# A hybrid scan and convolution layer: TensorE pinned to its written order, the latent convolution in pairs of quarters with re-laid buffers

## The chip, the cores and the metric

The kernel runs on one core of one Trainium2 chip. The metric is device time in microseconds (us) of one execution, as the median of several runs. The core has five engines with a queue of instructions each: TensorE (PE, matmul; its weight loads are shown apart as PEld), VectorE (DVE), ScalarE (ACT), GpSimd (POOL) and SyncE (SP), which here issues every DMA.

## The reference

One layer runs over 256 context tokens and 2048 latent tokens. Cut to what matters here:

```python
h = rms_norm(x, g_pre) * (1 + scale) + shift
u = h @ w_in                                        # 1024 -> 5664
z, xbc, dt_raw, ga, gb, gsil = split(u)
y_ssd, h_fin = ssd_branch(z, xbc, dt_raw, ...)      # bidirectional scan in chunks of 128 tokens
h = ga * sigmoid(gb)                                # conformer_branch
h = depthwise_conv(h, conv_w, conv_b)               # 31 taps along the rows of the grid
y_conf = silu(layer_norm(h, ln_g, ln_b)) * silu(gsil)
out = concatenate([y_ssd, y_conf]) @ w_out
return x + gate * rms_norm(out, g_post), h_fin
```

The context is a grid of 256 x 1, the latents one of 32 x 64; the convolution runs down the 32 rows, so along the latents it joins tokens that lie 64 apart. Within a scan chunk, `y_diag` is a masked, decayed product of 128 x 128 per head, `y_off` what the state so far adds, and `states` what the chunk adds to the state.

## The kernel before

The 2304 tokens are 18 tiles of 128, two of context and sixteen latent, worked in two halves (tiles 0 to 9, 10 to 17). Every large product is made of three matmuls on operands split into a high and a low part in the type float32r (`mm_cm`, L365: high x high, low x high, high x low, for eight k), each with a moving width of 512 or 256. Call a group of three a k-step. The tiles of these are `xp`, `gb`, `ga`, `sp` and, in the output product, `op`.

Each half goes through `xbc_phase` (the projection that feeds the scan, with a 5-tap convolution) and then through `post` (L862): eight `gab_unit`s (`gb` and `ga`, the gated input of the Conformer branch) and the `silu_unit`s (`sp`). While `post` runs, side work is interleaved by `interleave` and `merge` (L842, L49): after so many k-steps the generators of the scan and of the convolution are advanced by a step each. The scan, `pass_a(i)` (L640), is started for a new tile every seven steps. For tile i it loads rows of cumulated decay (`lb`, spread over all partitions), masks them on GpSimd (`mask`), takes exponentials on ScalarE (`decay`), adds the two directions and multiplies by C·B (`mix`), and then uses TensorE: transposes (`pb`, `px`), `diag` (tile `py`: eight matmuls per group g whose stationary operand is 64 columns wide, four of them for each half hq), `off` (`po`, 128 wide), and `state` (`pst`, split operands again). `carry` updates the state in `Sf`, `close` adds up and stores.

The Conformer convolution of the context is done on VectorE (`ctx_conv`, L572, tile `cg`). That of the latents is done on TensorE (`lat_conv(j)`, L595, for each of eight blocks of 128 channels). It loads the gated input as `cx` from the DRAM buffer `GL`, expands the taps `kd` into block-diagonal matrices in one of two buffers `kbuf` (four ScalarE copies for each of four quarters u, L614), runs eight matmuls of 64 columns for a quarter (tile `cp`), and evicts them with the bias into `cvv`, which is stored to `CVL`. The output stage (L1094 on) reads `CVL` back as `cn` (L1030), normalizes, transposes (`ct`), and multiplies by `w_out`.

PSUM has three banks under the tag "mm" for the large products and five under "ss" for all else. The order of instructions on each engine isn't that of the source: the program is built with a scheduler (`schedule_with_timeline_sim=True`, L1214) that reorders each engine's queue by its own estimate of when operands are ready. So TensorE's order around the side work is the scheduler's: in `post` it puts a small matmul wherever it takes its inputs to be there.

The lines that the steps of the prediction touch: L532 (store to `GL`), L608 (load of `cx`), L614 (expansion), L626 (`cp`), L631 (eviction), L636 (store to `CVL`), L712 (`py`), L719 (`po`), L725 to L727 (`pst`), L763 to L765 (`pb`), L688 (`px`), L665 (`el`, an exponential of `lb`), L668 (mask), L676 (decay), L680 and L681 (the two steps of `mix`), L531 and L542 (evictions of `ga` and `sp`), L1030 and L1033 (`cn` and its statistics).

## Time and profile before

| | |
|---|---|
| median of 3 runs | 1885.21 us (1884.33 to 1887.44) |
| profiled execution, its time | 1890.22 us |
| profiled execution, its span | 1888.5 us |
| mean granted TensorE clock | 0.989 |
| DVE busy, share of the span | 63% |
| ACT busy, share of the span | 44% |
| POOL busy, share of the span | 14% |
| DMA packets under 512 B | 85206 of 290400 |

The span runs from the first instruction to the last; 1.7 us lie around it in the execution's time. A row of the timeline gives the start, the duration, the engine, the line, the operation, the tile written and those read, the shapes, and how many instructions are merged in it; a bracket at its end is the time that the engine stood idle before it, and what ended that. A matmul's duration reaches into the next one, since matmuls are pipelined: the cost of one is the distance from its start to the next one's start. A matmul on plain 32-bit operands shows as two records, a transpose as one. A window's row gives, for a stretch of the span, its length, the busy time of PE, PEld, DVE, ACT and POOL (with instructions), the granted TensorE clock, the mean busy share of the 16 DMA engines, and GB/s.

### The profile page before, as it was taken

To read this page: it belongs to the slowest core of one execution; us is meant where nothing else is said; L and a number is where in the kernel's file an instruction comes from. 1 tells how busy PE (TensorE), PEld (TensorE's weight loads), DVE (VectorE), ACT (ScalarE), POOL (GpSimd) and SP (SyncE) were. 2 spreads that over 40 slices of the span, in tenths; PEclk is the share of its full clock that TensorE was granted. 3 is DMA by queue.
4 is the path that set the end of the run, shared out by engine and by line. 5 is a ranking of instruction groups with operands and counts; after the bars stand their busy time and mean duration, and the time that the engine had idled before them with its cause. 6 is when DMAs were issued, how large, how long until landed. Compare 5 with 4: busy or idle time off the path is not lost.

```text
span 1888.5 us, 26833 instructions
## 1 busy us (share of the span) xinstructions
PE 1827.4 (97%) x9739; PEld 1500.1 (79%) x9739; DVE 1192.4 (63%) x1699; ACT 839.9 (44%) x1786; POOL 264.6 (14%) x351
## 2 busy tenths in 40 slices
PE   7899999999999999999999998999999999999998
PEld 4788887787787888888877776767787888888886
DVE  2487877776545543586596758655438767776762
ACT  3647424443455441744356666664414323222321
POOL 0002001111111100100001111100003233333220
PEclk9999999999999999999999999999999999999999
DMA  8556665564686754445587888987887565555532
GB/s 299 213 199 214 216 217 187 169 219 154 206 274 222 229 204 162 162 154 198 186 184 220 213 228 226 246 213 201 248 262 237 182 183 168 160 171 168 177 104 75
DMA packets 290400, 375.29 MB, mean 199 GB/s; under 512 B 85206, under 2 KB 187478, under 8 KB 290268
## 3 DMA queue, kind: packets, MB, share of 16 engines
q1 hardware_dynamic: 290268, 373.58, 63.9%
q8 instruction: 77, 1.26, 0.3%
q14 instruction: 55, 0.45, 0.1%
HBM read 243.92 MB, written 129.59 MB: 198 GB/s over the span
## 4 chain that ended last, share of the span: by engine, by line
PE 60%; DMA 6%; issue 4%; ACT 3%; DVE 3%; SPq 1%; POOL 1%; POOLq 0%; DVEq 0%; ACTq 0%
PE op L1069 19%; PE sp L370 6%; PE sp L371 6%; PE sp L372 6%; DMA lb<-lt 4%; PE xp L372 2%; PE xp L371 2%; PE xp L370 2%; PE ga L370 1%; PE qo L976 1%; PE ga L372 1%; PE ga L371 1%; PE py L712 1%; PE gb L370 1%; PE gb L372 1%
## 5 line engine op out<-in xcount | busy, mean ns | idle before, releaser
L676 ACT ACTIVATE lb<-lb,WB 128x128 f32<-128x128 f32 x576 | 184.2, 391 | 150.9 <-POOL lb L668 149.0
L370 PE MATMUL sp<-hh,wh 128*128 128x512 f32 (+1 forms) x640 | 239.3, 374 | 1.9 <-DVE sth L542 1.9
L371 PE MATMUL sp<-hl,wh 128*128 128x512 f32 (+1 forms) x640 | 237.6, 371 | 0.0
L372 PE MATMUL sp<-hh,wl 128*128 128x512 f32 (+1 forms) x640 | 237.0, 370 | 0.0
L668 POOL TENSOR_SCALAR_AFFINE_SELECT lb<-lb 128x512 f32<-128x512 f32 x144 | 108.7, 759 | 751.8 <-ACT el L665 393.8
L370 PE MATMUL xp<-hh,wh 128*128 128x512 f32 (+1 forms) x480 | 178.0, 372 | 5.3 <-ACT wh L345 3.4
L371 PE MATMUL xp<-hl,wh 128*128 128x512 f32 (+1 forms) x480 | 178.2, 372 | 0.2 <-DVE hl L291 0.2
L372 PE MATMUL xp<-hh,wl 128*128 128x512 f32 (+1 forms) x480 | 178.1, 371 | 0.0
L467 DVE SCALAR_TENSOR_TENSOR cva<-raw,cwh,cva 128x1280 f32<-128x1280 f32 (+1 forms) x96 | 142.5, 1493 | 15.3 <-ACT cva L461 13.4
L370 PEld LDWEIGHTS sp<-hh,wh 128*128 128x128 f32 x640 | 121.1, 189 | 23.9 <-DVE sth L542 2.3
L372 PEld LDWEIGHTS sp<-hh,wl 128*128 128x128 f32 x640 | 121.1, 189 | 20.7 <-issue 0.2
L371 PEld LDWEIGHTS sp<-hl,wh 128*128 128x128 f32 x640 | 121.1, 189 | 20.3 <-issue 0.5
L370 PE MATMUL gb<-hh,wh 128*128 128x512 f32 (+1 forms) x320 | 121.5, 380 | 6.1 <-DVE gth L531 6.1
L370 PE MATMUL ga<-hh,wh 128*128 128x512 f32 (+1 forms) x320 | 120.2, 376 | 3.2 <-ACT gth L528 3.2
L371 PE MATMUL gb<-hl,wh 128*128 128x512 f32 (+1 forms) x320 | 119.4, 373 | 0.0
L372 PE MATMUL gb<-hh,wl 128*128 128x512 f32 (+1 forms) x320 | 119.3, 373 | 0.0
L372 PE MATMUL ga<-hh,wl 128*128 128x512 f32 (+1 forms) x320 | 118.3, 370 | 0.0
L371 PE MATMUL ga<-hl,wh 128*128 128x512 f32 (+1 forms) x320 | 118.2, 369 | 0.0
L582 DVE SCALAR_TENSOR_TENSOR cg<-cg,cv 128x256 f32<-128x256 f32 x240 | 112.3, 495 | 2.5
L542 DVE SCALAR_TENSOR_TENSOR sth<-sth,sp 128x512 f32<-128x512 f32 (+1 forms) x80 | 50.4, 630 | 96.0 <-ACT sth L541 96.0
L370 PEld LDWEIGHTS xp<-hh,wh 128*128 128x128 f32 x480 | 91.3, 190 | 22.0 <-ACT wh L345 4.1
L680 DVE TENSOR_TENSOR lb<-lb,lb 128x512 f32<-128x512 f32 x72 | 50.2, 697 | 88.6 <-ACT lb L676 55.8
(219 smaller groups left out, 3862.9 us busy)
## 6 DMA issues: line engine op xcount, KB each, us to landing
lb<-lt SPq DMA_DIRECT2D x144, 256.0 KB, 4.6
wr<-in_w_in SPq DMA_DIRECT2D x88, 256.0 KB, 4.9
whd<-wh SPq DMA_DIRECT2D x44, 512.0 KB, 3.2
wld<-wl SPq DMA_DIRECT2D x44, 512.0 KB, 4.6
wh<-whd SPq DMA_DIRECT2D x44, 512.0 KB, 5.7
wl<-wld SPq DMA_DIRECT2D x44, 512.0 KB, 5.6
xT<-xb SPq DMA_DIRECT2D x18, 512.0 KB, 5.6
yp<-yg SPq DMA_DIRECT2D x36, 256.0 KB, 4.8
```

Source lines behind the costliest of these rows:

```text
L370: T.matmul(ps[:, :BN], wh[:, k, :], hh[:, k, :], start=(k == 0), stop=False)
L371: T.matmul(ps[:, :BN], wh[:, k, :], hl[:, k, :], start=False, stop=False)
L372: T.matmul(ps[:, :BN], wl[:, k, :], hh[:, k, :], start=False, stop=(k == KT - 1))
L467: V.scalar_tensor_tensor(a[:, :n], raw[:, t:t + n], cwh[:, ct * 5 + t:ct * 5 + t + 1], a[:, :n], MUL, ADD)
L542: V.scalar_tensor_tensor(th, th, 1.0, ps[:, :BN], ADD, MUL)
L582: V.scalar_tensor_tensor(acc, g[:, t:t + 256], cv[:, w0 + t:w0 + t + 1], acc, MUL, ADD)
L668: G.affine_select(E[g, hq, d], E[g, hq, d], pattern=[[0, 4], [sg, P]], compare_op=ALU.is_ge, fill=NEG, base=0, channel_multiplier=-sg)
L676: S.activation(lb[:, h, :], lb[:, h, :], AF.Exp, bias=WB[:, i, c + h:c + h + 1])
L680: V.tensor_tensor(a, a, E[g, hq, 1], ADD)
L712: T.matmul(py[g][j * HD:(j + 1) * HD, q * P:(q + 1) * P], xt[g][:, h * HD:(h + 1) * HD], E[g, hq, 0][:, t, :], start=True, stop=True)
L976: T.matmul(po[:, q * P:(q + 1) * P], Sb[g][:, q * P:(q + 1) * P], ct[:, g, :], start=True, stop=True)
L1069: T.matmul(pso[n], lhs[:, k % 8, :], w[:, n * 512:(n + 1) * 512], start=(k == 0 and m == 0), stop=(k == 15 and m == 2))
```

## The change

1. TensorE's instructions go through a wrapper that, while `T.on` is set, ties each one behind the one written before it, so the scheduler can't move them. It is set over the interleaved stretch of both `post` phases. The other engines are still scheduled freely.
2. `pass_a` is cut into other steps. The two halves of a group's `diag` and its `off` now stand together; the two `px` stand with `pb`; masks, decays, sums and products of `mix` have steps of their own, ahead of the matmul that needs them. A step of `lat_conv` is called right behind `off(0)` and behind `state(1, 0)`. The first context tile to carry its state out gets ten steps instead of seven.
3. `lat_conv` is one generator over the eight blocks. It works in pairs of quarters, has four `kbuf` buffers instead of two and two `cx` buffers instead of one, and expands the taps of block j + 1 right after the pair of block j that used the buffers.
4. `GL` is split: the context part `GLC` as it was, the latent part `GLX` in the order in which `cx` lies in SBUF. So each `ga` block of latents is stored by four DMAs in pieces of 256 B, and `cx` is one DMA of whole rows. `CVL` is written as `cvv` lies (one DMA of whole rows instead of two in pieces of 256 B), and `cn` is read from it by two DMAs in pieces of 256 B, instead of one in rows of 4 KB.
5. The load of the initial state is issued earlier for the first use, `ctx_conv` and `gate_rows` get two empty steps ahead of their matmuls, and the step counts of the interleaving follow.

```diff
+class InOrder:
+    def __init__(self, tc, eng):
+        self.tc, self.eng, self.on = tc, eng, False
+
+    def _put(self, ins):
+        return self.tc.keep_in_program_order(ins) if self.on else ins
+
+    def matmul(self, *a, **k):
+        return self._put(self.eng.matmul(*a, **k))
...
-    V, S, G, T, DMA = nc.vector, nc.scalar, nc.gpsimd, nc.tensor, nc.sync
+    V, S, G, T, DMA = nc.vector, nc.scalar, nc.gpsimd, InOrder(tc, nc.tensor), nc.sync
...
-            DMA.dma_start(GL[j][:, o:o + BN], th)
+            if b == 0:
+                DMA.dma_start(GLC[j], th)
+                continue
+            r0 = (o - NCTX * P) // 64
+            for c4 in range(4):
+                DMA.dma_start(GLX[j][c4 * 32 + r0:c4 * 32 + r0 + BN // 64, :].rearrange("r (g w) -> g r w", w=64),
+                              th.rearrange("(g c) (r w) -> c g r w", c=4, w=64)[c4])
...
-        x = lp.tile([P, 32, 64], F32, tag="cx", name=f"cx{j}", bufs=1)
-        src = GL[j][:, 256:].rearrange("(g c) (r w) -> c r g w", c=4, w=64)
-        for c4 in range(4):
-            DMA.dma_start(x[c4 * 32:(c4 + 1) * 32], src[c4])
...
-        expand(0)
-        yield
-        for u in range(4):
-            kt = kbuf[u % 2]
-            ps = bank("ss", f"cp{j}_{u}")
...
-            if u < 3:
-                expand(u + 1)
-            yield
...
+        def load_g(j):
+            x[j] = lp.tile([P, 32, 64], F32, tag="cx", name=f"cx{j}", bufs=2)
+            DMA.dma_start(x[j].rearrange("p g w -> p (g w)"), GLX[j])
...
+        for j in range(8):
+            vt[j] = lp.tile([P, 32, HD], F32, tag="cvv", name=f"cvv{j}", bufs=1)
+            for v in range(2):
+                ps = [part(j, 2 * v + e) for e in range(2)]
+                for e in range(2):
+                    evict(j, 2 * v + e, ps[e])
+                if j < 7:
+                    if v == 0:
+                        load(j + 1)
+                    else:
+                        load_g(j + 1)
+                    for e in range(2):
+                        expand(j + 1, 2 * v + e)
+                else:
+                    pass
+                if v == 1:
+                    DMA.dma_start(CVL[j * P:(j + 1) * P, :], vt[j].rearrange("p r c -> p (r c)"))
+                yield
...
         diag(0, 0)
+        diag(0, 1)
         off(0)
-        state(0, 0)
-        weigh(1, 0)
-        mix(1, 0)
-        decay(1, 1)
-        yield
-        diag(0, 1)
-        state(0, 1)
-        carry(0)
-        weigh(1, 1)
-        mix(1, 1)
+        if cpg is not None:
+            next(cpg, None)
+        weigh(0, 1)
+        both(1)
+        yield
+        close(0)
+        state(0, 0)
+        times(1)
+        yield
+        carry(0)
+        state(0, 1)
+        weigh(1, 0)
...
-    interleave(post(0, 6), merge(scan(range(9)), 68, extra, 9 + 4 * 13), 90 * 8)
+    T.on = True
+    blocks = post(0, 6)
+    run(take(blocks, 40))
+    interleave(blocks, merge(scan(range(9)), 76, extra, 11 + 4 * 15), 90 * 8 - 40)
+    T.on = False
...
-    kbuf = [lp.tile([P, 8, P], F32, name=f"kbuf{u}") for u in range(2)]
+    kbuf = [lp.tile([P, 8, P], F32, name=f"kbuf{u}") for u in range(4)]
...
+    T.on = True
     run(take(blocks, 24))
-    interleave(take(blocks, 24), [sc_] * 4, 24)
-    interleave(take(blocks, 344), merge(sc_, 63, extra, 8 * 6 + 4 * 13), 344)
+    interleave(take(blocks, 16), [sc_] * 3, 16)
+    next(cpg)
+    interleave(take(blocks, 352), merge(sc_, 68, extra, 4 * 15), 352)
...
-        DMA.dma_start(n, CVC[i * P:(i + 1) * P, :] if i < 2 else CVL[(i - 2) * P:(i - 1) * P, :])
+        if i < NCTX:
+            DMA.dma_start(n, CVC[i * P:(i + 1) * P, :])
+        else:
+            for e in range(2):
+                DMA.dma_start(n[e * 64:(e + 1) * 64, :].rearrange("w (j c) -> w j c", c=64),
+                              CVL.rearrange("(j w) (r c) -> r w j c", w=64, c=64)[2 * (i - NCTX) + e])
```

On TensorE, in the second half, where the scan of tile 11 ends and that of tile 12 begins (the digits behind a name are tile, group and half; `cp2_1` is quarter 1 of block 2), there stood before, row by row:

```order
L626 MATMUL cp2_1_9725<-kbuf1_8336,cx2_9615 64x128 x8
L372 MATMUL ga1_4_4_9760<-hh4_7341,wl3104_1_9120 128x512
L712 MATMUL py111_9694<-lb11110_9470,xt111_9450 64x128 x2
L626 MATMUL cp2_2_9745<-kbuf0_8335,cx2_9615 64x128 x8
L712 MATMUL py111_9694<-lb11110_9470,xt111_9450 64x128 x2
L725 MATMUL pst1111_9771<-xwh1111_9640,bth11_9358 128x512
L726 MATMUL pst1111_9771<-xwl1111_9641,bth11_9358 128x512
L727 MATMUL pst1111_9771<-xwh1111_9640,btl11_9359 128x512
L763 MATMUL pb12_9779<-ident_209,bc12_9649 128x128 x2
```

Of the change, on the same engine, at the first `diag` of tile 12 (L77 is the wrapper's line, for whatever matmul):

```order
L77 MATMUL ga1_5_3_10095<-hl3_7188,wh3232_1_9610 128x512
L77 MATMUL ga1_5_3_10095<-hh3_7187,wl3232_1_9609 128x512
L77 MATMUL py120_10117<-lb12000_9736,xt120_10018 64x128 x4
L77 MATMUL py120_10117<-lb12010_9775,xt120_10018 64x128 x4
L77 MATMUL po120_10126<-bc12_9732,Sf0_266 128x128 x4
L77 MATMUL cp3_0_10132<-kbuf0_8391,cx3_10001 64x128 x8
L77 MATMUL cp3_1_10141<-kbuf1_8392,cx3_10001 64x128 x8
L77 MATMUL ga1_5_3_10095<-hh3_7187,wh3232_1_9610 128x512
```

Both halves of `py` and two quarters of `cp` stand in one place, where a half or a quarter stood by itself or was cut in two, with large matmuls between.

On ScalarE, at the expansion of the taps, there stood before (quarters 2 and 3 of block 2, whose `cp` row is in the first listing; what waits for PE waits until quarters 0 and 1 have read the same two buffers):

```order
L614 COPY kbuf0_8335<-kd2_9610 32x8x32 [waits PE_49]
L614 COPY kbuf0_8335<-kd2_9610 32x8x32 x3
L676 ACTIVATE lb13001_10128<-lb13001_10128,WB_255 128x128 [waits DMAHW6_49,Pool_49]
L665 ACTIVATE el121_9652<-lb12100_9858 64x256 [waits DMAHW7_49,DVE_49]
L614 COPY kbuf1_8336<-kd2_9610 32x8x32 [waits PE_49]
L614 COPY kbuf1_8336<-kd2_9610 32x8x32 x3
```

Of the change, on ScalarE, the expansion of quarters 2 and 3 of block 3, behind the cast for the first `pst` of tile 12:

```order
L753 CAST xwh1200_10065<-xw1200_10064 128x512 [waits DVE_49,PE_49]
L645 COPY kbuf2_8393<-kd3_9709 32x8x32 [waits PE_49]
L645 COPY kbuf2_8393<-kd3_9709 32x8x32 x3
L645 COPY kbuf3_8394<-kd3_9709 32x8x32 [waits PE_49]
L645 COPY kbuf3_8394<-kd3_9709 32x8x32 x3
```

The copies still wait for TensorE, but for the same quarters of the block before: a buffer is filled a block ahead of its use, no longer between two quarters of the same block.

More of the change, by code (lines that the diff above doesn't have):

```diff
@@ L85, in backbone_kernel @@
     ZS = [dram(f"zs{h}", [D, HT[h] * P]) for h in range(2)]
-    GL = [dram(f"gl{j}", [P, NT * P]) for j in range(KT)]
+    GLC = [dram(f"glc{j}", [P, NCTX * P]) for j in range(KT)]
+    GLX = [dram(f"glx{j}", [P, LAT]) for j in range(KT)]
     GS = [dram(f"gs{h}", [D, HT[h] * P]) for h in range(2)]
     CVC = dram("cvc", [NCTX * P, D])
-    CVL = dram("cvl", [LAT, D])
+    CVL = dram("cvl", [D, LAT])
     YP = [dram(f"yp{i}", [P, D]) for i in range(NT)]
@@ L623, in lat_conv, with part @@
+        def part(j, u):
             ps = bank("ss", f"cp{j}_{u}")
@@ L676, in decay, with both, times @@
                     S.activation(lb[:, h, :], lb[:, h, :], AF.Exp, bias=WB[:, i, c + h:c + h + 1])
-        def mix(g, hq):
-            a = E[g, hq, 0]
-            V.tensor_tensor(a, a, E[g, hq, 1], ADD)
-            V.tensor_tensor(a, a, cb[:, g, :].unsqueeze(1).to_broadcast([P, 4, P]), MUL)
+        def both(g):
+            for hq in range(2):
+                V.tensor_tensor(E[g, hq, 0], E[g, hq, 0], E[g, hq, 1], ADD)
+        def times(g):
+            for hq in range(2):
+                a = E[g, hq, 0]
+                V.tensor_tensor(a, a, cb[:, g, :].unsqueeze(1).to_broadcast([P, 4, P]), MUL)
         xt, px, py, pst, po = {}, {}, {}, {}, {}
@@ L766, in pass_a @@
         x_in(0)
-        mask(0, 0)
-        load_lb(0, 1)
+        x_in(1)
+        both(0)
+        load_lb(1, 0)
+        load_lb(1, 1)
         yield
@@ L797, in pass_a, with scan @@
         diag(0, 0)
+        diag(0, 1)
         off(0)
+        if cpg is not None:
+            next(cpg, None)
+        weigh(0, 1)
+        both(1)
+        yield
+        close(0)
         state(0, 0)
+        times(1)
+        yield
+        carry(0)
+        state(0, 1)
         weigh(1, 0)
-        mix(1, 0)
-        decay(1, 1)
-        yield
-        diag(0, 1)
-        state(0, 1)
-        carry(0)
-        weigh(1, 1)
-        mix(1, 1)
         yield
         diag(1, 0)
+        diag(1, 1)
         off(1)
+        keep(0)
+        weigh(1, 1)
+        yield
+        close(1)
+        yield
         state(1, 0)
-        keep(0)
-        close(0)
+        if cpg is not None:
+            next(cpg, None)
         yield
-        diag(1, 1)
+        carry(1)
         state(1, 1)
-        carry(1)
         yield
         keep(1)
-        close(1)
+        if st is not None:
+            state_out(0, Sf, lambda n: pa.tile([P, 512], F32, tag="yo", name=n, bufs=1))
+            yield
+            state_in(0, Sf, st)
         yield
-        if i == NCTX - 1:
-            state_out(0, Sf, lambda n: pa.tile([P, 512], F32, tag="yo", name=n, bufs=1))
-            state_in(0, Sf, big("sti0").rearrange("p (q n) -> p q n", n=P))
-            yield
-    def scan(tiles):
-        gens = [pass_a(i) for i in tiles]
-        live, t = [], 0
+    def scan(tiles, cpg=None):
+        gens = [(i, pass_a(i, cpg)) for i in tiles]
+        live, t, at = [], 0, 0
         while gens or live:
-            if gens and t % 7 == 0:
-                live.append(gens.pop(0))
+            if gens and t == at:
+                i, g = gens.pop(0)
+                live.append(g)
+                at += 10 if i == NCTX - 1 else 7
             for g in list(live):
@@ L925, in backbone_kernel @@
     cg = lambda name: lp.tile([P, D], F32, tag="cg", name=name, bufs=2)
-    extra = chain(f for j in range(4) for f in (lat_conv(2 * j, lp, kbuf), ctx_conv(j + 4, cg), lat_conv(2 * j + 1, lp, kbuf)))
-    sc_ = scan(range(9, NT))
+    extra = chain(ctx_conv(j, cg) for j in range(4, 8))
+    cpg = lat_conv(lp, kbuf)
+    next(cpg)
+    sc_ = scan(range(9, NT), cpg)
+    T.on = True
     run(take(blocks, 24))
-    interleave(take(blocks, 24), [sc_] * 4, 24)
-    interleave(take(blocks, 344), merge(sc_, 63, extra, 8 * 6 + 4 * 13), 344)
+    interleave(take(blocks, 16), [sc_] * 3, 16)
+    next(cpg)
+    interleave(take(blocks, 352), merge(sc_, 68, extra, 4 * 15), 352)
     run(sc_)
     run(extra)
+    run(cpg)
+    T.on = False
     ph_l.close()
```

102 lines of the change are left out of this document (56 added, 46 removed).

## The prediction

> **What bounds the kernel now.** I read the page first, then the busy time by stage, then who made TensorE wait in each stage, and last the timeline of TensorE around single groups of small matmuls. The sum is made against the profiled execution, whose span is the page's first line; 1.7 us around it make its time of 1890.22 us.
>
> ```profile
> span 1888.5 us, 26833 instructions
> 231.00:756.00 525.00, 513.80 (x2878) 428.29 (x2877) 317.69 (x538) 223.39 (x549) 48.99 (x77) 0.99 0.62 204
> 918.00:1362.00 444.00, 422.97 (x2472) 333.04 (x2471) 284.11 (x459) 259.03 (x572) 45.67 (x70) 0.98 0.81 218
> 1426.00:1888.50 462.50, 452.10 (x2182) 374.21 (x2181) 308.75 (x354) 135.21 (x276) 131.97 (x116) 0.99 0.53 162
> ```
>
> The three windows are the first `post`, the second `post`, and the output stage. TensorE (second number) is busy in nearly all of each; no other engine is near. So a microsecond saved on TensorE is one saved at the end, and one in which TensorE waits is one lost. The change touches the first two windows, 969 us, and the reading of `cn` in the third. Two things can be saved there: waits, and time in which TensorE counts as busy but does little. The waits of TensorE in the first and in the second window:
>
> ```profile
> PE gb L370 <- DVE gth L531: 6.1, 3, 4.7
> PE ga L370 <- ACT gth L528: 3.2, 2, 1.7
> PE sp L370 <- DVE sth L542: 1.9, 1, 1.9
> PE cp L626 <- ACT kbuf L614: 12.0, 6, 4.1
> PE px L688 <- issue: 3.5, 2, 2.5
> PE cp L626 <- DMA cx<-gl: 3.1, 1, 3.1
> PE px L688 <- PE pb L765: 0.8, 1, 0.8
> ```
>
> That is 11.2 us in the first and 19.4 us in the second, 30.6 us in all; what is left out is 0.5 us or less each.
>
> Now the hidden part. In a timeline the price of a group of small matmuls is read from the start of the last large one before it to the start of the second large one behind it, less two strides of a large one. First a group with a 64-column stationary operand (`py`, eight records, four matmuls) and one of 128 (`po`, eight records):
>
> ```profile
> 603.16 0.39 PE L371 MATMUL sp<-hl,wh 128*128 128x512 f32 x1
> ...
> 604.07 0.39 PE L372 MATMUL sp<-hh,wl 128*128 128x512 f32 x1
> 604.39 0.66 PE L712 MATMUL py<-lb,xt 128*64 128x128 f32 x8
> 604.98 1.16 PE L719 MATMUL po<-bc,Sf 128*128 128x128 f32 x8
> 605.89 0.48 PE L725 MATMUL pst<-xwh,bth 128*128 128x512 f32 x1
> 606.21 0.39 PE L726 MATMUL pst<-xwl,bth 128*128 128x512 f32 x1
> ```
>
> Four strides from 603.16 to 604.07 give 0.2275 us for a large matmul. From 604.07 to 606.21 are 2.14 us; less two strides, 1.685 us for `py` and `po`. What `po` costs is seen in the output stage, in groups of eight and of sixteen 128-column records:
>
> ```profile
> 1612.60 0.62 PE L1069 MATMUL op<-woh,yl 128*128 128x512 f32 x2
> 1613.06 1.95 PE L976 MATMUL qo<-ct,Sb 128*128 128x128 f32 x16
> 1614.76 0.71 PE L1069 MATMUL op<-woh,yh 128*128 128x512 f32 x2
> 1615.31 0.62 PE L1069 MATMUL op<-wol,yh 128*128 128x512 f32 x2
> ...
> 1624.29 0.62 PE L1069 MATMUL op<-woh,pl 128*128 128x512 f32 x2
> 1624.75 1.03 PE L1049 MATMUL ct<-ident,cn 128*128 128x128 f32 x8
> 1625.54 0.71 PE L1069 MATMUL op<-woh,ph 128*128 128x512 f32 x2
> 1626.09 0.39 PE L1069 MATMUL op<-wol,ph 128*128 128x512 f32 x1
> ```
>
> Sixteen take 2.71 less four strides, 1.80 us; eight take 1.80 less four strides of 0.23, 0.88 us: about 0.11 us a record and no constant. So the eight of `po` are 0.90 us, and 0.785 us are left for four matmuls of `py`. Sixteen matmuls of 64 columns in one group:
>
> ```profile
> 1166.92 0.39 PE L372 MATMUL gb<-hh,wl 128*128 128x512 f32 x1
> 1167.24 1.97 PE L626 MATMUL cp<-kbuf,cx 128*64 128x128 f32 x32
> 1169.14 0.50 PE L370 MATMUL gb<-hh,wh 128*128 128x512 f32 x1
> 1169.48 0.40 PE L371 MATMUL gb<-hl,wh 128*128 128x512 f32 x1
> ```
>
> 2.56 less 0.455 is 2.105 us. Twelve more matmuls cost 1.32 us more: 0.11 us each, and a **constant of 0.345 us** for each run of 64-column matmuls, whatever its length. It shows as longer strides when TensorE goes into the run and out of it. Groups of 128 columns don't pay it.
>
> The third loss is the clock. The five stretches of the two windows in which the granted clock was 0.50 (all follow waits of TensorE) sum up to this:
>
> ```profile
> sum 23.80, PE 18.66 PEld 14.82 DVE 17.32 ACT 15.63 POOL 2.86; mean PE 3.73 PEld 2.96 DVE 3.46 ACT 3.13 POOL 0.57
> ```
>
> 18.66 us of busy time at half speed would be 9.3 us at full speed. A busy time of matmuls is modelled and reaches past their work, so I take two thirds, 6.2 us, and keep 9.3 as the most.
>
> **The change, part by part.** *Whole bursts.* Counted in the order of the built programs, TensorE enters a run of 64-column matmuls (`py` or `cp`, anything else ends it) 99 times before: 69 of `py` alone, 27 of `cp` alone, 3 mixed. In the changed program it does so 52 times: 36 of `py`, where each group's two halves now follow one another, and 16 of `cp`, in pairs of quarters; eight of these follow a `po`. 47 runs at 0.345 are **16.2 us**. The trace shows no `po` followed by `cp`; such an entry costs between nothing and the full constant, so the gain is 16.2 to 19.0 us. I take the full constant, since leaving `py` for `po` was paid in full in the row above. The `pst` that no longer follow a burst cost nothing extra: the price was taken up to the second large matmul.
>
> *Four `kbuf`, two `cx`, a block ahead.* The 12.0 and 3.1 us go if the new lead covers the load and the copies. The copies of a pair stand on ScalarE behind the matmuls that read the same buffers a block earlier, and the next use is a tile later. A tile's share of the second `post`: 352 k-steps of three strides are 240 us, and nine tiles' small work comes on top: twelve `pst` at 0.2275, some 46 records and pairs of `pb`, `px`, `po` and `py` at 0.11, 32 matmuls of `cp` at 0.11 and four constants, 12.7 us a tile or 114 us. Seven of 68 scan steps of these 354 us are **36 us a tile**. The copies and loads of a block are a few us of that:
>
> ```profile
> lb<-lt SPq DMA_DIRECT2D x144, 256.0 KB, 4.6
> ...
> cx<-gl SPq DMA_DIRECT2D x32, 256.0 KB, 6.2
> ...
> cn<-cvl SPq DMA_DIRECT2D x16, 512.0 KB, 4.0
> L676 ACT ACTIVATE lb<-lb,WB x576: 383/388/413, 156.8 to 1302.7; 128x128 f32<-128x128 f32 x192
> ...
> L668 POOL TENSOR_SCALAR_AFFINE_SELECT lb<-lb x144: 628/635/1882, 155.4 to 1301.2; 128x512 f32<-128x512 f32 x144
> L665 ACT ACTIVATE el<-lb x136: 400/415/423, 278.6 to 1300.7; 64x256 f32<-64x256 f32 x136
> L680 DVE TENSOR_TENSOR lb<-lb,lb x72: 673/692/1132, 160.3 to 1303.2; 128x512 f32<-128x512 f32 x72
> ```
>
> `cx` lands in 6.2 us and is issued half a tile, 18 us, ahead. Both waits go: 15.1 us.
>
> *Written order.* A matmul that waits now holds up all the large ones written behind it; the scheduler can't put others in front. The tightest chain to a `py` starts when the previous tile's `py` frees the `lb` buffers: load 4.6, four `el` at 0.415, two masks at 0.635, eight exponentials at 0.388, then two sums and two products on DVE at 0.69: 13.4 us, of 36. That leaves 23 us for queueing on SP, ACT and DVE, so I count no wait for it. The waits for `gth` and `sth` (11.2 us) come from DVE and ACT, whose order the scheduler still sets; I let half remain, and half of the 4.3 us at `px`, whose two groups now stand with `pb` but still need free banks. So of the waits about **8 us stay and 22.6 go**; the bounds are none left and all 30.6 left. Of the clock's 6.2 us, shorter waits leave 2: **4.2 us**.
>
> [...]
>
> *The buffers.* Pieces of 256 B move rather than go: `cx` loads and `cvv` stores of the second `post` become whole rows, the `GLX` stores (four DMAs for one, 128 for 32, in both `post`) and the `cn` loads (two for one) take them over. In the second `post` a block has 10 DMAs (8 stores, one load, one store of `cvv`) where it had 8, with fewer pieces; DMA is at 0.81 there, and nothing behind these on SP is closer to its use than the 23 us above. In the first `post` it is at 0.62. I count nothing for both. In the output stage DVE waits for `cn` already, but TensorE doesn't:
>
> ```profile
> 1607.91 1.29 DVE L1033 BATCH_NORM_STATS2 bs<-cn 128x6 f32<-128x512 f32 x2 [3.63 <-DMA cn<-cvl]
> ...
> 1612.16 0.15 DVE L997 TENSOR_SCALAR yms<-pm 128x1 f32<-128x1 f32 x1
> 1618.93 0.38 PE L1003 MATMUL pm<-ident,yr 128*128 128x128 f32 x2
> ```
>
> The nearest need of TensorE behind that wait in DVE's queue is `yms`, whose root `pm` needs at 1618.93, 6.6 us after `yms` ends. Two loads of 256 KB in such pieces should land as `cx` did, in 6.2 us instead of 4.0: 2.2 us later, covered. Zero. Empty steps and the earlier state load: zero, `post` has work there.
>
> *Sum.* 16.2 + 22.6 + 4.2 = 43.0 us. Span 1888.5 to 1845.5, the execution 1890.2 to 1847.2. The median of the runs lies 5.0 us under the profiled execution (1885.2), so I forecast **1842 us**.
>
> **Rivals.** *The waits stay* (0.13). The other engines' order is still the scheduler's guess, so as many us of waiting turn up at other matmuls. Only the constants are saved: 1885.2 - 16.2 = 1869. For it speaks that 11.2 us of waits name DVE and ACT; against it, that half of the total named the two buffers that are doubled.
>
> *Written order stalls* (0.09), slower. One mechanism: the chain to `py`, or the bank that `close` frees one step ahead of `pst`, is late in every tile, and nothing may pass. If each of 18 tiles waits once as long as the longest wait above, 4.7 us, that is 84.6 us against 53.0 saved with all old waits gone: 31.6 more, 1917. It decides from 2.9 us a tile on. For it: ACT and DVE are in-order and their queues mix this work with evictions. Against it: the 23 us of slack, and nothing like it in the trace.
>
> *`cn` is late* (0.06). The price starts at 6 us more latency.
> [...] Were the halves to land one after the other, at 6.2 us each, `cn` would be 8.4 us later, 2.4 beyond its cover in each of 16 tiles, 38 us, and the result 1880. The trace has four loads of 32 partitions issued together landing in 6.2 us, so it is improbable.
>
> *No effect* (0.03): new waits eat the constants to within 0.2% (3.8 us, about what can be told from no change). That the order isn't changed at all is excluded by the listings.
>
> **How the numbers follow.** Forecast 0.66. Its own range: with all waits and 9.3 us of clock gone and no entry from `po`, 16.2 + 2.8 + 30.6 + 9.3 = 58.9, 1826; with the waits of the first window all left, 1850. With the second case at 1869 and 3 us of spread the range is 1826 to 1872, which leaves out about 2 in 10: the slower case, `cn`, no effect, and the forecast's edges. Faster: 0.66 + 0.13 + 0.06 and 0.03 for more than the range holds, 0.88; same 0.03; slower 0.09.
>
> **What would show it.** Right: 52 runs of `py` or `cp` with a constant near 0.345; no wait of TensorE for `kbuf` or `cx`; the two `post` together 43 us shorter; fewer stretches at half clock; the output stage unchanged. Wrong: TensorE waits at `py`, `pst` or `pb` (tiles, since all have the line of the wrapper) for DVE, ACT or `lb`, once a tile; or at `ct` or `pm` for DVE in the output stage; or a `cp` behind a `po` that costs more than the constant.

## The result and the profile after

The changed kernel takes 1916.9 us (median of 4 runs, 1911.5 to 1918.7), the kernel before 1885.1 beside it: a ratio of 1.0155, 95% interval 1.0137 to 1.0172. It is slower by 32 us, where 1842 was forecast.

The profiled execution after takes 1917.63 us. Of its page the first line, and of its windows the same three stages as before, cut at the first large matmul of each:

```profile
span 1915.8 us, 26956 instructions
```

```profile
231.40:780.80 549.40, 532.70 (x3005) 451.90 (x3003) 332.38 (x559) 235.35 (x570) 55.18 (x81) 0.99 0.61 200
921.00:1433.90 512.90, 481.18 (x2776) 394.40 (x2775) 304.88 (x487) 271.79 (x593) 55.95 (x79) 0.97 0.68 220
1433.90:1908.60 474.70, 457.02 (x2181) 374.61 (x2181) 298.21 (x348) 133.15 (x274) 121.04 (x115) 0.99 0.60 156
```

Cut in the same way (first `gb` of a half, first `xp` of the second half, first `op`, start of TensorE's last matmul), the kernel before has 546.7, 507.9 and 455.2 us. So the two `post` phases together, which were to be 43 us shorter, are 7.7 us longer, and the output stage, which was to stay, is 19.5 us longer: 27.2 of the 27.3 us by which the span grew.

The waits of TensorE in these stages, in the order of the stages:

```profile
PE sp L77 <- DVE sth L568: 12.2, 5, 3.1
PE gb L77 <- DVE gth L551: 2.7, 1, 2.7
PE px L80 <- DVE gr L594: 1.8, 1, 1.8
...
PE cp L77 <- ACT xt L743: 23.6, 7, 5.0
PE cp L77 <- ACT sb L789: 5.1, 2, 3.7
PE px L80 <- ACT sb L789: 3.1, 3, 1.4
...
PE pm L77 <- POOL yr L145: 12.7, 9, 4.1
```

`cp` no longer waits for `kbuf` or `cx`, as forecast. But the two `post` now wait 16.7 and 31.8 us, 48.5 in all. Before, it was 32.3: the 30.6 of the prediction and four waits of 0.5 us or less, 1.7 together. The output stage waits 12.7 us at `pm`, where it had no wait.

What was to be saved on runs of 64-column matmuls was saved. A group with both halves of `py`, a `po` and two quarters of `cp`, on TensorE's timeline of the second `post`:

```profile
1005.85 0.39 PE L77 MATMUL gb<-hh,wl 128*128 128x512 f32 x1
1006.17 1.09 PE L77 MATMUL py<-lb,xt 128*64 128x128 f32 x16
1007.20 1.16 PE L77 MATMUL po<-bc,Sf 128*128 128x128 f32 x8
1008.28 1.97 PE L77 MATMUL cp<-kbuf,cx 128*64 128x128 f32 x32
...
1010.52 0.40 PE L77 MATMUL gb<-hl,wh 128*128 128x512 f32 x1
```

It costs 4.67 less two strides, 4.215 us. The eight records of `po` cost 0.90 together, and 24 matmuls at 0.11 bring it to 3.54; the rest, 0.675, is two constants of 0.34. So a `cp` behind a `po` pays the full constant, the end of the range that was taken. Next, all distances between TensorE's starts were summed, and each one that holds a wait or takes 0.4 us or more (at half clock it is 0.427) was counted with a large matmul's 0.2275 us at most. These sums fell from 531.2 to 524.5 us in the first `post` and from 481.4 to 472.4 in the second: **15.7 us**, forecast 16.2.

How a wait of the first `post` comes about:

```profile
630.11 0.94 SPq L703 DMA_DIRECT2D lb<-lt  x2
...
635.77 1.72 ACT L712 ACTIVATE el<-lb 64x256 f32<-64x256 f32 x4 [8.38 <-DMA lb<-lt]
...
640.28 0.58 ACT L567 ACTIVATE sth<-sp 128x512 f32<-128x512 f32 x1
...
641.07 0.68 DVE L568 SCALAR_TENSOR_TENSOR sth<-sth,sp 128x512 f32<-128x512 f32 x1
...
641.80 0.50 PE L77 MATMUL sp<-hh,wh 128*128 128x512 f32 x1 [3.06 <-DVE sth L568]
```

ACT stands still for 8.38 us at `el` until a load of `lb` lands. The eviction `sth` stands behind it, and TensorE waits for that eviction's bank. No `GLX` store is near: the last of the first `post` left SP at 501 us, and before this load SP issued weights (`wr`, `whd`, `wld`) and stores of `sth`. In the second `post` the same chain ends at `cp`:

```profile
1206.33 2.58 SPq L557 DMA_DIRECT2D glx<-gth  x4
...
1209.01 1.04 SPq L703 DMA_DIRECT2D lb<-lt  x2
...
1211.35 1.09 PE L77 MATMUL cp<-kbuf,cx 128*64 128x128 f32 x16
1213.50 0.84 ACT L712 ACTIVATE el<-lb 64x256 f32<-64x256 f32 x2 [4.56 <-DMA lb<-lt]
...
1215.63 1.07 ACT L743 COPY xt<-px 128x512 f32<-128x512 f32 x2
...
1216.27 1.34 PE L77 MATMUL cp<-kbuf,cx 128*64 128x128 f32 x16 [3.83 <-ACT xt L743]
```

The third quarter runs at once, the fourth waits: its bank is one that `px` of the next tile held, and the copy that frees it, `xt`, stands on ACT behind `el`. `px` had ended at 1206.6 us, and still ACT, idle from 1208.9, didn't take `xt` ahead of `el`: it keeps to its order. The `lb` load was issued as soon as four `GLX` stores had left SP.

In the output stage a ring turns. Its rows before (`bs` of this tile, at 1607.91, is in the prediction) and after:

```profile
1597.64 2.03 DVE L982 TENSOR_REDUCE zr<-z 128x128 f32<-128x1024 f32 x1
1599.70 0.38 SPq L968 DMA_DIRECT2D z<-zs  x1
...
1601.24 0.38 SPq L1030 DMA_DIRECT2D cn<-cvl  x1
...
1622.97 2.02 DVE L982 TENSOR_REDUCE zr<-z 128x128 f32<-128x1024 f32 x1
```

```profile
1589.70 2.01 DVE L1054 TENSOR_REDUCE zr<-z 128x128 f32<-128x1024 f32 x1
...
1591.73 0.38 SPq L1040 DMA_DIRECT2D z<-zs  x1
...
1593.27 1.93 SPq L1106 DMA_DIRECT2D cn<-cvl  x2
...
1601.87 1.29 DVE L1110 BATCH_NORM_STATS2 bs<-cn 128x6 f32<-128x512 f32 x2 [7.03 <-DMA cn<-cvl]
...
1606.95 0.49 PE L77 MATMUL pm<-ident,yr 128*128 128x128 f32 x2 [1.09 <-POOL yr L145]
...
1616.38 2.03 DVE L1054 TENSOR_REDUCE zr<-z 128x128 f32<-128x1024 f32 x1
```

A ring is a chain that ends where it began, one tile later. Here `zr` frees the buffer of `z`; on SP the load of `z` goes, behind it `y`, behind that `cn`; `cn` lands, DVE works on it and comes to the next `zr`. From the issue of `cn` to `bs` were 6.67 us and are 8.60; from `bs` to `zr` were 15.06 and are 14.51. A round took 25.3 us, TensorE's time for a tile, and this one takes 26.7.

### The profile page after: what moved, and what is told of

Read it like the earlier page. It is cut to its first block, busy times and chain, and to the rows that moved or that the text cites. A ratio compares the mean times of both kernels' runs of the same rounds, so it can differ in the third digit from the quotient of the medians.

```text
span 1915.8 us, 26956 instructions
## 1 busy us (share of the span) xinstructions
PE 1825.3 (95%) x9739; PEld 1513.2 (79%) x9739; DVE 1186.5 (62%) x1699; ACT 836.4 (44%) x1786; POOL 263.0 (14%) x353
## 4 chain that ended last, share of the span: by engine, by line
PE 61%; DMA 14%; DVE 10%; ACT 6%; issue 5%; POOL 1%; SPq 1%; POOLq 0%; DVEq 0%; ACTq 0%
PE xp L77 15%; PE sp L77 15%; PE gb L77 8%; PE ga L77 8%; PE op L77 7%; DMA lb<-lt 6%; DMA cn<-cvl 4%; ACT lb L723 2%; ACT kbuf L645 2%; PE pst L77 2%; PE py L77 1%; PE po L77 1%; DVE y L1050 1%; ACT el L712 1%; DMA wm<-in_w_mod 1%
## 5 line engine op out<-in xcount | busy, mean ns | idle before, releaser
L77 PE MATMUL sp<-hh,wh 128*128 128x512 f32 (+1 forms) x640 | 242.8, 379 | 12.2 <-DVE sth L568 12.2
L77 PE MATMUL sp<-hl,wh 128*128 128x512 f32 (+1 forms) x640 | 238.7, 373 | 0.0
L77 PE MATMUL sp<-hh,wl 128*128 128x512 f32 (+1 forms) x640 | 238.4, 372 | 0.0
L715 POOL TENSOR_SCALAR_AFFINE_SELECT lb<-lb 128x512 f32<-128x512 f32 x144 | 113.6, 792 | 698.9 <-ACT el L712 384.7
L77 PE MATMUL xp<-hh,wh 128*128 128x512 f32 (+1 forms) x480 | 178.4, 373 | 4.3 <-ACT wh L365 3.0
L77 PE MATMUL xp<-hh,wl 128*128 128x512 f32 (+1 forms) x480 | 178.3, 372 | 0.0
L77 PE MATMUL xp<-hl,wh 128*128 128x512 f32 (+1 forms) x480 | 178.3, 372 | 0.0
L77 PEld LDWEIGHTS sp<-hh,wh 128*128 128x128 f32 x640 | 122.5, 191 | 35.9 <-DVE sth L568 14.5
L77 PEld LDWEIGHTS sp<-hh,wl 128*128 128x128 f32 x640 | 122.1, 191 | 21.2
L77 PEld LDWEIGHTS sp<-hl,wh 128*128 128x128 f32 x640 | 122.6, 192 | 20.0
L77 PE MATMUL gb<-hh,wh 128*128 128x512 f32 (+1 forms) x320 | 121.8, 381 | 2.7 <-DVE gth L551 2.7
L77 PE MATMUL ga<-hh,wh 128*128 128x512 f32 (+1 forms) x320 | 120.7, 377 | 0.0
L610 DVE SCALAR_TENSOR_TENSOR cg<-cg,cv 128x256 f32<-128x256 f32 x240 | 118.1, 512 | 2.4
L77 PE MATMUL gb<-hl,wh 128*128 128x512 f32 (+1 forms) x320 | 119.4, 373 | 0.0
L77 PE MATMUL gb<-hh,wl 128*128 128x512 f32 (+1 forms) x320 | 119.1, 372 | 0.0
L77 PE MATMUL ga<-hl,wh 128*128 128x512 f32 (+1 forms) x320 | 118.5, 370 | 0.0
L77 PE MATMUL ga<-hh,wl 128*128 128x512 f32 (+1 forms) x320 | 118.4, 370 | 0.0
L1052 ACT ACTIVATE z<-y 128x1024 f32<-128x1024 f32 x18 | 19.1, 1062 | 226.6 <-DVE y L1051 226.6
L712 ACT ACTIVATE el<-lb 64x256 f32<-64x256 f32 x136 | 56.4, 415 | 126.9 <-DMA lb<-lt 105.2
```

The lines of the kernel that those rows point to most:

```text
L77: return self._put(self.eng.matmul(*a, **k))
L610: V.scalar_tensor_tensor(acc, g[:, t:t + 256], cv[:, w0 + t:w0 + t + 1], acc, MUL, ADD)
L712: S.activation(el[g][rs, q:q + 2, :], E[g, hq, 0][rs, j::2, :], AF.Exp)
L715: G.affine_select(E[g, hq, d], E[g, hq, d], pattern=[[0, 4], [sg, P]], compare_op=ALU.is_ge, fill=NEG, base=0, channel_multiplier=-sg)
L1052: S.activation(z, y, AF.Square)
```

## The experiments

Each of these is the changed kernel with one edit, unless it says otherwise. Stages in us, cut as above, from one profiled execution each; the medians are of 4 to 7 runs beside the kernel before on the same chip (1884.5 to 1885.3). The profiled execution of the kernel before is 5 us above its median, so a stage's difference to it is only good to some us; the columns are best read against the second row.

| run | first post | second post | output | median | ratio, 95% interval |
|---|---|---|---|---|---|
| before | 546.7 | 507.9 | 455.2 | 1885.1 | |
| after | 549.4 | 512.9 | 474.7 | 1916.9 | 1.0155 (1.0137 to 1.0172) |
| e1 `CVL` as before | 548.8 | 522.7 | 455.3 | 1906.4 | 1.0116 (1.0101 to 1.0131) |
| e2 pair moved | 547.7 | 522.3 | 474.8 | 1927.0 | 1.0232 (1.0193 to 1.0270) |
| e3 `GL` as before | 538.3 | 508.8 | 474.1 | 1904.7 | 1.0106 (1.0089 to 1.0122) |
| e4 e1 and e2 | 549.4 | 507.6 | 455.5 | 1893.1 | 1.0049 (1.0033 to 1.0064) |
| e5 `lb` a step ahead | 548.0 | 507.9 | 472.0 | 1911.7 | 1.0154 (1.0133 to 1.0176) |
| e6 e1 and e3 | 538.2 | 518.3 | 455.1 | 1892.9 | 1.0049 (1.0024 to 1.0074) |
| e7 e1, e2, e3 | 538.9 | 498.9 | 456.5 | 1874.9 | 0.9947 (0.9929 to 0.9966) |
| e8 before, new buffers | 548.7 | 507.5 | 475.2 | 1912.1 | 1.0151 (1.0130 to 1.0171) |
| e9 `lb` by GpSimd | 529.8 | 517.2 | 477.9 | 1907.2 | 1.0125 (1.0092 to 1.0159) |
| e10 e7 and e9 | 530.1 | 496.2 | 458.2 | 1869.1 | 0.9922 (0.9907 to 0.9937) |
| e11 `z`, `y` otherwise | 549.7 | 512.9 | 474.1 | 1917.9 | 1.0179 (1.0162 to 1.0197) |
| e12 `py` cut by `po` | 544.5 | 520.1 | 475.6 | 1920.8 | 1.0187 (1.0162 to 1.0211) |
| e13 `z`, `y` by ACT | 548.8 | 512.2 | 458.5 | 1898.5 | 1.0077 (1.0058 to 1.0096) |
| e14 e2, e3, e9, e13 | 530.2 | 504.9 | 458.2 | 1878.1 | 0.9964 (0.9949 to 0.9980) |

One part of the change needed no run. A build in which `T.on` is never set gives the same program as the changed kernel, with every instruction of all five engines in the same place. In the kernel before, TensorE steps back behind the written order at 13 places in the two `post`, and nowhere else there. So the pinning is empty here: what moved TensorE's instructions is the new order of the steps.

### The buffers: e1, e3, e6, e8

e1:

```diff
...
-                    DMA.dma_start(CVL[j * P:(j + 1) * P, :], vt[j].rearrange("p r c -> p (r c)"))
+                    for h in range(2):
+                        c0 = j * P + h * 64
+                        DMA.dma_start(CVL[:, c0:c0 + 64].rearrange("(r w) c -> w r c", w=64), vt[j][h * 64:(h + 1) * 64])
...
-            for e in range(2):
-                DMA.dma_start(n[e * 64:(e + 1) * 64, :].rearrange("w (j c) -> w j c", c=64),
-                              CVL.rearrange("(j w) (r c) -> r w j c", w=64, c=64)[2 * (i - NCTX) + e])
+            DMA.dma_start(n, CVL[(i - NCTX) * P:(i - NCTX + 1) * P, :])
```

> The changed kernel, with CVL stored and cn loaded as in the kernel before: two stores of 256-B pieces a block, one load of whole rows a tile. Theory A (the output stage is 19.5 us longer because the cn loads land 3.3 us later, DVE waits for them and yr comes late for pm): the output stage goes back to about 454 us between the first and the last op, the wait of pm for yr goes from 12.7 us to under 1, and the time from 1917 to about 1897. Rival (the output stage is longer for another reason, such as a new order on DVE): pm still waits and the time stays within 4 us of 1917.

The output stage is back at 455.3 us, and `pm` has no wait: theory A is right on the stage. The time fell by 10.5 us only, not 20, since the second `post` grew by 9.8, with 37.6 us of waits of `cp` for `xt` where there were 23.6. Storing `cvv` in pieces costs there what the change had saved.

e3, the same for the gated input:

```diff
...
-            if b == 0:
-                DMA.dma_start(GLC[j], th)
-                continue
...
-                DMA.dma_start(GLX[j][c4 * 32 + r0:c4 * 32 + r0 + BN // 64, :].rearrange("r (g w) -> g r w", w=64),
...
+            DMA.dma_start(GL[j][:, o:o + BN], th)
...
-            DMA.dma_start(x[j].rearrange("p g w -> p (g w)"), GLX[j])
+            src = GL[j][:, 256:].rearrange("(g c) (r w) -> c r g w", c=4, w=64)
+            for c4 in range(4):
+                DMA.dma_start(x[j][c4 * 32:(c4 + 1) * 32], src[c4])
```

> The changed kernel, with the gated input stored in GL and cx loaded as in the kernel before: one store instead of four for a ga block, four loads instead of one for cx. Theory C (the 96 more issues on SP make the lb loads late, and with them ACT, the evictions sth and gth and the xt copies): the waits in the first post fall by about 9 us and those in the second by about 10, time about 1898. Rival (SP has room, the lateness comes from the step order alone): both post phases stay within 3 us, time 1913 to 1920.

The first `post` is 11.1 us shorter, its waits of TensorE down from 16.7 to 8.9 us; the second is 4.1 shorter, not 10. So theory C holds for the first and is half a miss for the second. e6 joins the two edits:

> The changed kernel with all three buffers (GL, cx's load, CVL and cn) as in the kernel before; the step order, the pairs and the four kbuf stay. If the stages add up: first post 538 us (as with GL alone), second 519 (513, plus 10 for the stores of CVL in pieces, less 4 for GL), output stage 455: time about 1893. Rival (the two edits of the second post compete for the same DMA time and SP issues, and the sum is worse): second post 525 or more, 1900 and up.

1892.9 us, and the stages add up to within a microsecond. What the change does besides the buffers is thus worth nothing yet: 0.5% slower than before, although the constants of 47 runs are saved. e8 is the other half, the new buffers in the kernel before and nothing else:

```diff
-    GL = [dram(f"gl{j}", [P, NT * P]) for j in range(KT)]
+    GLC = [dram(f"glc{j}", [P, NCTX * P]) for j in range(KT)]
+    GLX = [dram(f"glx{j}", [P, LAT]) for j in range(KT)]
...
-    CVL = dram("cvl", [LAT, D])
+    CVL = dram("cvl", [D, LAT])
...
```

> The kernel before with the new buffers alone (GLC and GLX with four stores a block, cx as one load, CVL as cvv lies, cn by two loads of 256-B pieces); its step order, its quarters and its two kbuf stay. If the buffers cost by themselves what they cost in the changed kernel: first post 11 us longer (558), second 6 shorter (502), output stage 19 longer (475), time about 1909. Rival (the stores of GLX cost only where the new step order leaves the lb loads little lead): first post within 3 us of 547, time about 1898.

1912.1 us, a ratio of 1.0151, as much as the whole change. The output stage grew by 20.0 us. But the first `post` grew by 2.0 us, not 11: there the rival is right, and the `GLX` stores cost only beside the new step order. The second `post`, forecast 6 us shorter, stayed as it was (507.5).

### The ring of the output stage: e11, e13

e11 was to open the ring with a third buffer for `z` and the `y` loads on GpSimd:

```diff
-        DMA.dma_start(y.rearrange("p q l -> p (q l)"), YP[i])
-        z = p1.tile([P, 8, P], F32, tag="z", name=f"z{i}", bufs=2)
+        nc.gpsimd.dma_start(y.rearrange("p q l -> p (q l)"), YP[i])
+        k = order.index(i)
+        z = (p1 if k % 3 else zp[0]).tile([P, 8, P], F32, tag="z", name=f"z{i}", bufs=2 if k % 3 or zp[0] is p1 else 1)
...
```

> The changed kernel with a third buffer for z in the output stage and the y loads issued by GpSimd, so that the cn loads on SP no longer stand behind loads of z and y that wait for DVE; the cn loads stay two of 256-B pieces. Theory G (a ring sets the period of a tile: zr frees z, the z and y loads let cn out, cn lands 8.6 us later, and 14.5 us of DVE's work lead to the next zr; 26.7 us instead of 25.3): with the ring open the output stage goes back to about 457 us though the loads take as long, time about 1900. Rival (the latency of cn costs wherever it stands in the queue, because ct frees the one cn buffer late): 474 us, time 1917.

Nothing changed, and the timeline says why:

```profile
1618.02 2.03 DVE L1055 TENSOR_REDUCE zr<-z 128x128 f32<-128x1024 f32 x1
...
1620.07 0.38 SPq L1041 DMA_DIRECT2D z<-zs  x1
1620.54 1.82 SPq L1107 DMA_DIRECT2D cn<-cvl  x2
```

`z` still left when `zr` ended, 0.02 us later, and `cn` right behind: the edit had not opened the ring, and the run tells nothing of it. e13 takes both loads off SP's queue:

```diff
-        DMA.dma_start(y.rearrange("p q l -> p (q l)"), YP[i])
+        nc.scalar.dma_start(y.rearrange("p q l -> p (q l)"), YP[i])
...
-        DMA.dma_start(z, chan_slice(ZS, i))
+        nc.scalar.dma_start(z, chan_slice(ZS, i))
```

> The changed kernel with the loads of z and y in the output stage issued by ScalarE, so that on SP the cn loads stand behind the load of stl at the latest (its buffer is free 3 us before zr ends); cn itself stays two loads of 256-B pieces. Theory G again (the ring from zr over the z and y loads to cn and back sets the period of a tile at 26.7 us): cn is issued about 2.9 us earlier, the ring takes 23.8 us, less than the 25.3 of TensorE, the output stage goes from 474 to about 457 us, time about 1900. Rival (not the place in the queue but the latency of cn behind its own ct is what is too long): 474 us, 1917.

The output stage takes 458.5 us, `pm` has no wait, and from the third tile on a tile takes from `op` to `op` what it took before, 25.3 us for the twelve in the middle. What the stage takes beyond 455.2 lies in the first two tiles. The loads are as slow as in the changed kernel:

```profile
1611.73 0.37 ACTq L1040 DMA_DIRECT2D z<-zs  x1
1612.26 1.30 SPq L1106 DMA_DIRECT2D cn<-cvl  x2
...
1622.27 1.29 DVE L1110 BATCH_NORM_STATS2 bs<-cn 128x6 f32<-128x512 f32 x2 [4.87 <-DMA cn<-cvl]
```

Theory G is shown: the ring over SP's queue, not the latency alone, made the stage longer, by 16 of the 19.5 us.

### Who makes the two post wait: e2, e4, e5, e7, e9, e10, e14

e2 moves the second pair:

```diff
         state(0, 1)
+        if cpg is not None:
+            next(cpg, None)
         weigh(1, 0)
...
         state(1, 0)
-        if cpg is not None:
-            next(cpg, None)
```

> The changed kernel, with the second pair of quarters of each block behind state(0, 1) instead of state(1, 0), so that its two banks were last used by po and by the first pair of the same tile, and no longer by px of the next tile. Theory B (in the second post the fourth quarter waits for the bank that the next tile's xt copy frees, 23.6 us, and the waits bring half clock behind them): the waits of cp go to under 6 us, the second post gets about 25 us shorter, the time is about 1892. Rival (ACT is late because the lb loads are late, and TensorE, bound to a fixed order, will wait for ACT at another matmul): cp waits less, but px, pst, py or pb wait more, and the time stays within 6 us of 1917.

The wait for `xt` at `cp` is gone, and the second `post` is 9.4 us longer all the same. Its longest waits:

```profile
PE cp L77 <- ACT sb L789: 9.9, 5, 4.3
PE pst L77 <- DVE yg L804: 5.8, 3, 3.8
PE cp L77 <- DVE Sf L783: 4.4, 3, 2.1
PE pb L80 <- ACT sb L789: 4.3, 3, 2.8
```

The rival is right about the waits: TensorE waits for ACT and DVE at other matmuls. The time, 1927.0 us, is 10 us above 1917, where it had 6 at most. With `CVL` as before too (e4) it is not:

> The first two edits together: CVL and cn as before, and the second pair behind state(0, 1). If theories A and B are right and add up, 1917 less 20 less 25, about 1872, faster than the kernel before by 13 us. If B's rival is right, about 1897; if both rivals are, 1917.

There the same move makes the second `post` 15.1 us shorter than in e1, but 1893 us is 21 more than expected, since the gain only makes good e1's loss. With all three edits (e7):

> The same with the second pair behind state(0, 1) as well. With CVL as before that move made the second post 15 us shorter than without it, with CVL as changed 9 us longer. If the layout of CVL decides it, the second post is about 504 us and the time about 1878, 7 us faster than the kernel before; if the move only reshuffles the waits, the second post is 515 or more and the time 1889 or more.

It is 19.4 us shorter than in e6, 1874.9 us, 0.5% faster than before. So where the pair stands matters, and which way depends on the other transfers.

e5 gave the `lb` loads of the second `post` a longer lead in the written order, and to make room `cx` went back to one buffer:

```diff
         load_lb(0, 1)
         yield
+        if lbx:
+            yield
...
         decay(0, 1)
+        if lbx:
+            load_lb(1, 0)
+            load_lb(1, 1)
...
```

> The changed kernel; for the tiles of the second post alone the lb loads stand one step further ahead of the masks (an empty step behind the loads of group 0; those of group 1 one step earlier, in two buffers of their own per direction, for which cx has one buffer again). Theory D (ACT stands still at el until the lb loads land, the xt copies behind it free the bank of the fourth quarter late): ACT's idle time before el for lb in the second post falls from 35 us to under 10, the waits of cp for xt from 23.6 to under 6, the second post from 513 us to about 490, time about 1894. Rival (the bank comes late because of how many ACT and DVE instructions stand between px and the cp that needs its bank, whatever lb does): cp still waits over 15 us and the time stays within 6 us of 1917. The first post is the control: within 2 us.

ACT's idle time for `lb` there was 40.5 us, not under 10, the waits of `cp` for `xt` 19.0. The earlier step did not make SP issue the loads early enough: at 1168.3 us, for one, a pair left behind four `GLX` stores as before, and ACT waited 4.69 us for it. So e5 doesn't test theory D. e9 takes the loads to another queue:

```diff
-                DMA.dma_start(lb.rearrange("p h l -> p (h l)"),
+                nc.gpsimd.dma_start(lb.rearrange("p h l -> p (h l)"),
```

> The changed kernel with the 144 lb loads issued by GpSimd instead of SP. Theory F (on SP the lb loads stand in line behind stores that wait for DVE and ACT, the GLX stores above all; ACT then stands still at el, and the xt copies and the evictions behind it come late): ACT's idle time before el for lb falls from 70 us in the first post and 35 in the second to a third of that or less, the waits of TensorE in the two from 48 us to about 25, time about 1893. Rival (on GpSimd the loads stand behind masks that wait for el in turn, or the chain is as long anyway): waits and time as they are, 1911 to 1923, or slower.

What ended ACT's idle time ahead of work on `lb` in the first `post`, in the kernel before, in the changed kernel and in e9:

```profile
  DMA lb<-lt: 43.1, 17
```

```profile
  DMA lb<-lt: 69.8, 14
```

```profile
  DMA lb<-lt: 13.1, 7
```

The first `post` is 19.6 us shorter (529.8), with 3.8 us of waits left; 3.6 us of that are lost ahead of it, where the first such loads are issued. Theory F is right there. In the second it is not borne out: ACT's idle time for `lb` only fell from 35.3 to 27.5 us, `cp` waits 29.9 us for `xt`, and the stage is 4.3 us longer. One rival was not tested by itself: a load of `lb` also waits for DVE's sums (L727) to free its buffer. Of SP's waiting in the changed kernel 45 us in each `post` name these sums. e10 puts it on top of e7:

> The kernel of the run with all three edits (buffers as before, second pair behind state(0, 1)), with the lb loads issued by GpSimd as well. By theory F the remaining waits of its second post, 24 us, fall by half: about 1862. By the rival 1875, as without it.

1869.1 us, of the versions run the fastest: 0.8% faster than before, interval 0.6 to 0.9%. Against e7 the first `post` gains 8.8 us and the second 2.7, while 4.8 are lost ahead of the first and 1.7 in the output stage. The second keeps 8.8 us of waits at `cp` and has 9.0 at `ga` for loads of `wh` and `wl`. e14 is e10 with the new `CVL` and the open ring:

> The kernel of the 1869 us run (GL as before, second pair behind state(0, 1), lb loads issued by GpSimd), but with CVL and cn as changed, and z and y issued by ScalarE so that the ring in the output stage is open. If the stores of CVL in whole rows are worth 10 us in the second post here too: second post about 486 us, output stage 458, time about 1862. Rival (with the pair moved, CVL as changed makes the second post longer, as it did when only that pair was moved): second post 510 or more, time 1885 or more.

Neither: the second `post` takes 504.9 us, 8.7 more than in e10. With the pair moved the new `CVL` costs there, with the pair where the change put it, it saves. No run settles why.

### The constant: e12

```diff
         diag(0, 0)
+        off(0)
         diag(0, 1)
-        off(0)
...
         diag(1, 0)
+        off(1)
         diag(1, 1)
-        off(1)
```

> The changed kernel with po written between the two halves of py, so that TensorE goes into a run of 64-column matmuls 78 times instead of 52; nothing else is added. By the constant of 0.345 us, paid whatever stands on the other side: the groups of the two post phases cost 9.0 us more, time about 1926. Rival (next to po, and not to a large matmul, the entry costs nothing): time 1917. What the waits do is told apart by the price of the groups in the timeline, 0.345 us more for py, po, py than for py, po.

```profile
613.33 0.39 PE L77 MATMUL sp<-hh,wl 128*128 128x512 f32 x1
613.65 0.66 PE L77 MATMUL py<-lb,xt 128*64 128x128 f32 x8
614.24 1.16 PE L77 MATMUL po<-bc,Sf 128*128 128x128 f32 x8
615.32 0.66 PE L77 MATMUL py<-lb,xt 128*64 128x128 f32 x8
...
616.25 0.40 PE L77 MATMUL sp<-hl,wh 128*128 128x512 f32 x1
```

2.92 less two strides is 2.465 us: 0.90 for `po`, 0.88 for eight matmuls, 0.685 left, two constants where the uncut group has one (2.13 us). Summed over both `post` as above, the distances grew by 9.7 us for 26 runs, 0.37 each. The time grew by 3.9 only, since the waits of the first `post` fell: they go up and down by several us with any edit.

## Why the prediction was wrong

**Right.** TensorE bounds all three stages of the kernel before; in the changed one it no longer sets the pace of the output stage. The constant of 0.345 us and the 16.2 us (15.7 measured), with the full price behind `po`. The waits for `kbuf` and `cx` went. Nothing waits for `py` in the changed kernel, as the chain of 13.4 us of 36 had said.

**"About 8 us stay and 22.6 go" failed, by 40 us.** 48.5 us stay, 16.2 more than before. The step that failed is the one under "Written order": it followed the chain to `py`, found 23 us of slack, and stopped. It did not ask what else stands on ACT behind the first link. That link waits for a load, ACT keeps to its order, and `xt` and `sth`, which free banks, stand behind. The kernel before had the sign: ACT stood still for 43.1 us in its first `post` and 26.9 in its second until `lb` loads landed, so these came late for ACT even then. That the `lb` loads on SP make ACT late is shown for the first `post` (e9, 19.6 us). In the second the bank of the fourth quarter is shown to matter only with `CVL` as before (e4, e7).

**"4.2 us of clock" failed with it.** Steps between large matmuls of 0.427 us instead of 0.2275 rose from 22 to 54 in the two `post`: 6.4 us lost, not 4.2 gained. With 15.7 saved and 16.2 more of waits that makes 6.9 us, of 7.7 measured.

**"Pieces of 256 B move: I count nothing" failed twice.** Of the 96 more store issues 48 stand in the first `post`; without them it is 11.1 us shorter (e3), though they cost that only together with the new steps (e8: 2.0). And the output stage was 19.5 us longer. There the latency grew about as forecast, 1.93 us more from issue to `bs` where 2.2 were forecast, but by luck: the 4.0 us is the landing of a single `cn` load of the latents, the first, ahead of the ring. In the ring it was 6.67 and became 8.60, not 4.0 and 6.2. What failed is the cover: 6.6 us between `yms` and `pm` in one tile. The ring had 0.55 us of slack a round (15.06 to 14.51 us), so each round falls behind by what the latency adds beyond that. From `zr` to `zr` it was 25.3 us in every tile of the loop; now it is 28.4, 27.3 and 27.5, then 25.2 to 27.3. The first three rounds use up the 6.6 us. From `op` to `op` the first two tiles take 2.6 us more than before, the next two what they took before, the ten after them 11.0 more, and a later one, where `pm` waits 4.1 us, 5.9 more: 19.5 in all.

**The rivals.** "Written order stalls" gave 1917 us, which was measured, but not by its mechanism: no wait of 2.9 us or more in every tile, none for the chain to `py`, and the written order itself is empty as a constraint. Its number is a coincidence; what it said for itself, that ACT and DVE work in order with evictions between, is what the changed kernel's trace shows: ACT, idle from 1208.9 us, took `xt` only behind `el`, and DVE in the output stage, idle until `bs` at 1601.87 us, took `yms`, whose `pm` had ended at 1597.13, only at 1606.12. "The waits stay" had the place right, other matmuls, but not the size. "`cn` is late" named the place of most of the loss, at 0.06; its price was to start at 6 us more latency, and 1.93 were enough.

Were the halves of `cn` to land one after the other, it was to cost 38 us. In the tile of the rows above the second load left 0.64 us behind the first and landed 1.45 us behind it (1600.32 and 1601.77 us, by the trace's landing times), 7.9 us after it left. So in that tile the halves ran side by side, and this price was not paid.

**Still open.** Why the place of the second pair and the layout of `CVL` change the second `post` by 9 to 19 us with either sign. The waits there change their matmul with each edit, so a chain of several engines' queues is likely; no run showed it link by link. Nor does a run show how much of the lateness of `lb` in that stage is the queue and how much the buffer that DVE frees.

## What to carry to other kernels

Room at one place of one tile is a stock and not a rate: before a latency is called hidden, look for the ring that it is part of, over buffers and over a queue, and compare the slack of a round with what is added. Before a chain is called slack, list what stands behind its waiting link on the same in-order engine, and whose banks those instructions free. A store cut into four costs its issues on the queue that also carries the loads which others wait for: here four `GLX` stores took 2.58 us of SP (the rows at 1206.33 us), and without them the first `post` was 11.1 us shorter (e3; beside the old steps they cost 2.0 us, e8). Another queue for these loads was worth more here (1907.2 us, e9) than an earlier step (1911.7 us, e5).

## What the runs showed of the hardware

In the changed kernel's trace half clock did not go by the length of a single wait. TensorE after a wait of 2.83 us (the one of 3.06 us is the last row of the first `post`'s chain, above):

```profile
545.22 0.79 PE L77 MATMUL sp<-hh,wh 128*128 128x512 f32 x1 [2.83 <-DVE sth L568]
545.81 0.63 PE L77 MATMUL sp<-hl,wh 128*128 128x512 f32 x1
546.24 0.63 PE L77 MATMUL sp<-hh,wl 128*128 128x512 f32 x1
```

Here the matmuls follow at 0.43 us, at a granted clock of 0.50; behind the wait of 3.06 us they follow at 0.23. By the granted clock's record the traces of the kernel before and of the changed one have 17 stretches at half clock from the first `post` to the last matmul, 12 of 3.41 us and 5 of 6.83, and within a trace all of them start a multiple of 3.41 us apart. Cut into pieces of 3.41 us from these starts, the two traces show:

| clock in a piece | clock in the next | pieces | TensorE's idle time in the piece |
|---|---|---|---|
| full | half | 17 | 1.94 to 3.41 us |
| full | full | 935 | at most 1.82 us |
| half | half | 5 | 0.66 to 2.75 us |
| half | full | 17 | at most 0.48 us |

The 2.83 us put 2.17 into one piece; the 3.06 were split by a piece's edge into 1.39 and 1.68. So in these traces waits of nearly the same length came out differently by where they fell, and with 48.5 us of waits the time at half clock in the two `post` went from 23.9 to 41.0 us. What sets the clock beyond these numbers was not shown.

A TensorE run of 64-column matmuls paid its constant next to 128-column `po` groups as next to large ones: two took 0.675 us in the group with `cp`, two 0.685 us in e12, 0.34 each.
